# A streaming gradient kernel: one store of each three issued from a second queue, beside a load

## The chip, the cores and the metric

The kernel runs on one core of one Trainium2 chip. The metric is the device time of one execution in microseconds (us), given as the median of several executions. Ratios are the mean time of one kernel's fast runs over the mean time of the other's fast runs of the same rounds, so they are not quite the ratio of the medians quoted beside them. A 95% interval stands behind them where it matters. All profiles below are of executions in the fast state, at a granted clock of 1.00.

## The reference

```python
def setup_inputs():
    return {"x": np.random.randn(8192, 8192).astype(np.float32)}

def reference(x):
    return np.gradient(x, axis=1)
```

Inside a row each output is half the difference of the two neighbours. At the two ends of a row it is the plain difference of the last two elements. The input is 268.44 MB and the output is 268.44 MB; there is little arithmetic beside this traffic.

## The kernel before

The 8192 rows are cut into 32 tiles. A tile has 128 partitions with two whole rows each, which is 64 KB per partition and 8.4 MB in all. Three slots of on-chip memory (SBUF) hold tiles; tile i lives in slot i % 3, and the result is written over the input in the same slot. GpSimd (POOL) computes the row ends, VectorE (DVE) the inside, and either of them places the ends. All loads and all stores are issued by SyncE (SP) on one queue, in the order load, load, load, store, store, store.

```python
x_sets = x.rearrange("(s p t) m -> s p (t m)", p=P, t=R)      # P = 128, R = 2
slots = [pool.tile([P, SH + W], f32, ...) for k in range(NB)]  # NB = 3, W = 2 * 8192

def load(i):
    b = slots[i % NB]
    ins = nc.sync.dma_start(out=b[:, SH : SH + W], in_=x_sets[i])
    loads.append(chain(i, ins, *([stores[i - NB]] if i >= NB else [])))  # waits for the slot's store

for i in range(NB):
    load(i)
for i in range(nsets):                       # nsets = 32
    # ... POOL: ends; DVE: the inside, in place; POOL or DVE: place the ends ...
    ins = nc.sync.dma_start(out=out_sets[i, ...], in_=b[...])
    stores[i] = chain(i, ins, placed)
    if i % NB == NB - 1:                     # after the third store of a group
        for k in range(i + 1, min(i + 1 + NB, nsets)):
            load(k)
```

I call tiles 3g, 3g+1 and 3g+2 a group, with a first, second and third load and store. Each transfer is spread over 16 DMA engines; in the packet records of the trace each engine moves 8 of its 128 partitions, one 64 KB packet per partition. I call these packets rows 0 to 7 of the engine.

## Time and profile before

| | before |
|---|---|
| time, median of 3 runs | 1247.18 us |
| span of the profiled execution | 1245.0 us |
| VectorE busy | 554.8 us, 45% |
| DMA engines busy, mean | 99.8% |
| one group (three loads, three stores), nine groups | 115.96 to 116.68 us, mean 116.3 |

The timeline of one group of the kernel before (start in us, duration or span of the line in us, engine, what; in brackets the idle time of the engine before it and what ended it):

```profile
273.61 39.05 SPq L94 DMA_DIRECT2D out_dram<-slot  x3
275.23 0.20 POOL L70 TENSOR_TENSOR ends<-slot 128x4 f32<-128x4 f32 x1 [1.65 <-DMA slot<-in_x_dram]
...
294.59 0.20 POOL L70 TENSOR_TENSOR ends<-slot 128x4 f32<-128x4 f32 x1 [19.16 <-DMA slot<-in_x_dram]
...
312.11 0.19 POOL L92 COPY slot<-ends 128x4 f32<-128x4 f32 x1 [17.32 <-DVE slot L81]
...
313.93 0.34 SPq L60 DMA_DIRECT2D slot<-in_x_dram  x1
```

The second and third tile of the group become ready for POOL at 275.23 and 294.59, one transfer of 19.3 us apart. The issues of the three stores span 39.05 us from 273.61 on, and the last of them ends at 312.66. When the third is issued, the first two stores still have work for the engines: the loads were done at about 294.2, and two stores are 38.6 us. So the third store arrives a whole transfer before it can start. That reserve is why the engines have no gaps.

The waits of the SP queue itself say the same from another side (what SP waited for: total us, times, longest us):

```profile
SPq L94 <- DVE slot L92: 525.7, 21, 55.9
SPq L60 <- DMA out_dram<-slot: 373.2, 29, 19.2
SPq L94 <- POOL slot L92: 298.8, 12, 36.7
```

SP waits nearly all the time, and none of it costs anything as long as issued work is waiting at the engines.

### The profile page before, as it was taken

What the parts mean: (1) busy time and instruction counts of PE and PEld (TensorE: products, weight loads), DVE (VectorE), ACT (ScalarE), POOL (GpSimd) and SP (SyncE); (2) the same over time, 40 slices, a digit from 0 to 9 for tenths busy, and PEclk for the clock granted to TensorE, in tenths of its full rate; (3) what the DMA queues carried; (4) which work ended last, traced back from release to release, by engine and by line L of the source; (5) the groups of instructions that cost most, each with busy time, mean ns of one, the idle gap of its engine ahead of it and who ended that gap; (6) DMA issues with size and microseconds to landing.
All of it is one profiled execution on the core that took longest, in us unless ns stands there. A gap on an engine that the chain in (4) does not pass through costs nothing.

```text
span 1245.0 us, 241 instructions
## 1 busy us (share of the span) xinstructions
DVE 554.8 (45%) x54; POOL 8.8 (1%) x48
## 2 busy tenths in 40 slices
DVE  2850483079009603850582079009603840591083
POOL 0000000000000000000000000000000000000000
DMA  9999999999999999999999999999999999999999
GB/s 404 438 436 419 425 438 438 438 438 438 434 427 421 436 438 438 436 438 432 432 419 438 436 438 432 436 434 432 423 436 436 436 438 436 430 427 430 436 411 404
DMA packets 9361, 536.88 MB, mean 431 GB/s; under 512 B 1040, under 2 KB 1040, under 8 KB 1040
## 3 DMA queue, kind: packets, MB, share of 16 engines
q1 hardware_dynamic: 9360, 536.88, 99.8%
q14 instruction: 1, 0.01, 0.0%
HBM read 268.44 MB, written 268.44 MB: 431 GB/s over the span
## 4 chain that ended last, share of the span: by engine, by line
another core or an unknown queue 74%; DVE 18%; DMA 3%; issue 2%; POOL 1%; SPq 0%; POOLq 0%
DVE slot L81 18%; DMA slot<-in_x_dram 3%; POOL ends L70 0%; POOL slot L92 0%; SPq L60 0%; DVE slot L92 0%; POOLq L127 0%
## 5 line engine op out<-in xcount | busy, mean ns | idle before, releaser
L81 DVE CUSTOM_DVE_ANT_0 slot<-slot 128x16382 f32<-128x16382 f32 (+1 forms) x33 | 551.3, 16706 | 667.9 <-POOL ends L70 667.9
L70 POOL TENSOR_TENSOR ends<-slot 128x4 f32<-128x4 f32 x32 | 6.3, 198 | 988.8 <-DMA slot<-in_x_dram 988.8
L92 DVE COPY slot<-ends 128x4 f32<-128x4 f32 (+1 forms) x21 | 3.6, 172 | 0.7
L92 POOL COPY slot<-ends 128x4 f32<-128x4 f32 x12 | 2.3, 190 | 207.9 <-DVE slot L81 207.9
L116 POOL MEMSET const-bfloat16-1.0<- 128x1 bf16 x1 | 0.1, 102 | 0.0
L116 POOL MEMSET const-uint8-127<- 128x1 uint8 x1 | 0.1, 102 | 0.0
L116 POOL MEMSET const-float32-0.0<- 128x1 f32 x1 | 0.1, 99 | 0.2 <-issue 0.2
L116 POOL MEMSET const-float32-1.0<- 128x1 f32 x1 | 0.1, 99 | 0.0
## 6 DMA issues: line engine op xcount, KB each, us to landing
out_dram<-slot SPq DMA_DIRECT2D x2, 4096.0 KB, 20.2
slot<-in_x_dram SPq DMA_DIRECT2D x32, 58.0
out_dram<-slot SPq DMA_DIRECT2D x31, 40.3
```

The costliest lines, as they stand in the source:

```text
L70: ins = nc.gpsimd.tensor_sub(out=ends[:, i, :, :], in0=xin[:, :, 1 : m : m - 2], in1=xin[:, :, 0 : m - 1 : m - 2],)
L81: ins = nc.vector._custom_dve(dve_ops.TENSOR_TENSOR_REDUCE_SUB_MAX, out=b[:, c0:c1], in0=b[:, SH + c0 + 1 : SH + c1 + 1], in1=b[:, SH + c0 ...
L92: ins = placer.tensor_copy(out=res[:, :, 0 : m : m - 1], in_=ends[:, i, r : r + nr, :])
L116: nc = _bacc.Bacc("TRN2", target_bir_lowering=False, num_devices=1)
```

## The change

The intent is to let a store run beside the last load of its group, and so to have reads and writes in flight together. The first store of each group goes on the ScalarE (ACT) queue, where it does not have to stand behind the third load. At the end, the last two loads are moved ahead of store 29, which is ready by then, and store 29 runs on the ACT queue beside load 31.

```diff
+    n3 = (nsets - 2) // NB * NB                       # 30
+    next_loads = {i: range(i + 1, i + 1 + NB) for i in range(NB - 1, n3 - NB, NB)}
+    next_loads[n3 - 2] = range(n3, nsets)             # loads 30, 31 right after store 28
...
-                ins = nc.sync.dma_start(
+                queue = nc.scalar if i < n3 and (i % NB == 0 or i == n3 - 1) else nc.sync
+                ins = queue.dma_start(
                     out=out_sets[i, :, r * m : (r + nr) * m], in_=b[:, r * m : (r + nr) * m]
                 )
                 stores[i] = chain(i, ins, placed)
+                if i == n3 - 1:
+                    ... # store 29 waits until load 30 has landed
-            if i % NB == NB - 1:
-                for k in range(i + 1, min(i + 1 + NB, nsets)):
+            if i in next_loads:
+                for k in next_loads[i]:
                     load(k)
```

More of the change, by code (lines that the diff above doesn't have):

```diff
@@ L4 @@
 import concourse.tile as tile
-from concourse import bass_utils, dve_ops
+from concourse import bass_utils, dve_ops, mybir
 from concourse._compat import with_exitstack
@@ L61, in load @@
         loads.append(chain(i, ins, *([stores[i - NB]] if i >= NB else [])))
+    n3 = (nsets - 2) // NB * NB
+    assert nsets - 2 == n3
+    next_loads = {i: range(i + 1, i + 1 + NB) for i in range(NB - 1, n3 - NB, NB)}
+    next_loads[n3 - 2] = range(n3, nsets)
     with tc.manual_schedule():
@@ L97 @@
                 stores[i] = chain(i, ins, placed)
+                if i == n3 - 1:
+                    landed = mybir.DependencyInfo(mybir.DependencyClass.Sync, mybir.DependencyReason.DATA)
+                    tc.add_manual_dep(ins.ins, loads[n3].ins.name, landed, reason="beside the last load")
                 at = [halved]
-            if i % NB == NB - 1:
-                for k in range(i + 1, min(i + 1 + NB, nsets)):
+            if i in next_loads:
+                for k in next_loads[i]:
                     load(k)
```

## The prediction

> **What bounds the kernel now.** I began with the page's busy shares, its queue table and its chain.
>
> ```profile
> DVE 554.8 (45%) x54; POOL 8.8 (1%) x48
> ...
> DMA packets 9361, 536.88 MB, mean 431 GB/s; under 512 B 1040, under 2 KB 1040, under 8 KB 1040
> ...
> q1 hardware_dynamic: 9360, 536.88, 99.8%
> ```
>
> VectorE works 45% of the span; the one DMA queue keeps its 16 engines busy 99.8% of it. So this is a copy kernel: 268.44 MB in, 268.44 MB out, with the arithmetic beside it. The chain is of little use here: 74% of it is put down to an unknown queue, because the semaphores of the slots are reused.
>
> Next I asked for exact cycles of six transfers (three loads, three stores), cut from one tile's first POOL operation to that of the third tile after it.
>
> ```profile
> core 0: us, DVE busy (x) POOL busy (x), PEclk, DMA share, GB/s
> 139.84:255.87 116.03, 52.01 (x5) 0.78 (x4) 1.00 1.00 434
> 255.87:371.99 116.12, 51.84 (x4) 0.97 (x5) 1.00 1.00 433
> 953.95:1070.23 116.28, 52.02 (x5) 0.79 (x5) 1.00 1.00 433
> ```
>
> The DMA share (fifth number after the window) is 1.00 and the rate 433 to 434 GB/s. The packet records say why nothing is left: nearly every packet is a whole 64 KB row, takes 2.418 us (the least and the median; the mean is 2.425), and the next starts 3 ns before it ends, so the pitch is 2.415 us. Each engine has 8 rows of a transfer, so a transfer is 8 x 2.415 = 19.32 us and a cycle 6 x 19.32 = 115.9 us against the 116.03 measured. Loads and stores have the same pitch.
>
> Floor of the whole: 64 tile transfers x 8 rows x 2.415 = 1236.5 us per engine. Add 1.75 us before the first packet, 1.3 us from the last packet to the span's end, and the 2.1 us by which the run (1247.06) exceeds the span (1245.0): 1241.6 us. The kernel stands 5.5 us, 0.4%, above it. Any ordering that moves the same bytes by the same packets lives above 1241.6.
>
> Where the 5.5 us lie, from packets longer than 2.418: an average of 3.65 us per engine, of which 0.6 in the first packets, 1.1 near 41 to 62 us, and the rest in short stretches of up to 0.4 us, mostly in the last packet of a group's third load, just before the first store. The slowest engine lost more than the average, 5.6 us. The other visible hole is at the end:
>
> ```profile
> 1186.42 17.23 DVE L81 CUSTOM_DVE_ANT_0 slot<-slot 128x16382 f32<-128x16382 f32 x1 [59.81 <-POOL ends L70]
> 1203.68 0.17 DVE L92 COPY slot<-ends 128x4 f32<-128x4 f32 x1
> 1203.88 19.93 SPq L94 DMA_DIRECT2D out_dram<-slot  x3
> 1205.53 0.20 POOL L70 TENSOR_TENSOR ends<-slot 128x4 f32<-128x4 f32 x1 [19.14 <-DMA slot<-in_x_dram]
> ...
> GB/s 874 2185 874 437 874 437 0 0 0 0 0 0 0 437 437 437 0 437 0 0 0 0 0 0 0 0 0 0 0 0 0 4806 1748 437 0 0 0 0 0 0
> ```
>
> Store 30 is issued at 1203.88 and its packets start at 1204.72. The last line is the window 1200 to 1206 us in 40 slices by packet starts: almost none between 1202.0 and 1204.6. Twelve engines idle 1.4 to 2.4 us there by the packet records. But the last load's slowest engine ends at 1205.05, after store 30 is there: that engine never waits. All engines finish within 0.2 us of each other at 1243.7.
>
> **What the Trainium skill says.** "DMA: Bandwidth & Descriptors", section "Issuing engines are not separate DMA queues": transfers issued from several engines run on the same 16 DMA engines and interleave, and only issue time is saved. So the ACT queue brings no bandwidth. The trace before has one queue, so it cannot confirm; issue time is 0.34 us a transfer and hidden. Section "Queues, rings and completion order": each engine takes turns between the queues it has work for, packet by packet. I use this for the order of the shared stretch; no run shows it yet. Section "Where 436 GB/s comes from": a ceiling of 435.2 GB/s for the 16 ports. The trace agrees: 16 x 65,536 B / 2.415 us = 434 GB/s. Section "Latency and other measured facts": HBM-to-HBM copies reach a full 214 GB/s each way, so 428 in sum. That speaks against a load and a store overlapping to double the rate, and the trace here has no mixed stretch to test it.
>
> **The change, part by part.** Nothing is removed or added in work: VectorE and POOL have the same 54 and 48 instructions in the same order, and bytes and packet sizes stay. Eleven of 33 store issues move to ACT: ten first stores and store 29.
>
> Part 1, the first store beside the third load. Before, store 3 (issued at 157.57) queued behind load 5. Now it shares the engines with load 5 from about 158.4. The two need 2 x 19.32 = 38.64 us in either order, so store 3 still lands near 197.8, but load 5 lands there too instead of at 178.5. Sum for the engines: 0. The cost is in slack: tile 5 is now ready 19.3 us later, while only store 4 is queued to cover it, and SP issues load 6 only after store 5. Working of that wait, from the slowest engine's last packet of the load to the first packet of store 5: packet end to landing 0.41 (1205.05 to 1205.46), to POOL 0.07, POOL start to store issue 157.57 - 139.84 = 17.73, issue to first packet 0.84 (1203.88 to 1204.72). Sum 19.05 us. Store 4 covers 19.32. Margin 0.27 us, where the kernel before has a whole transfer (some 19 us). So the slowest engine should just not idle, but engines that are ahead by more than 0.27 us will wait, in each of ten groups. Before, a delay on one engine and a delay on another never added up; now each group starts its last store together. Summing the longest excess packet per group (1.0 + 0.3 + 1.1 + 0.1 + 0.3 + 0.2 + 0.4 + 0.8 + 0.8 + 0.8 + 0.7) gives 6.5 us against 5.6 on the slowest engine: about +1 us.
>
> Part 2, taking turns. Each shared stretch goes from a load packet to a store packet 8 times, where before it was once a group. If the excess before a first store (0.17 us per group averaged over engines, first group left out) is the price of that switch, it would be 7 more switches x 0.17 x 10 = 12 us. The next transition, store to load, has no excess packets at all, and some groups show none at load to store either, so I give this a weight of one in six: +2 us.
>
> Part 3, the end. Loads 30 and 31 come straight after store 28, and store 29, ready by then, shares the engines with load 31. Store 30 is computed during that stretch. The hole of about 2 us on most engines closes, but the slowest engine had none; its lead over the others was lost by only 0.3 us (1205.05 against 1204.72). Worth -0.3 us, up to -1.5 if the load is spread evenly.
>
> Sum: +1 + 2 - 0.3, and for the uncertain excesses of the first group (1.1 us in the stretch where store 0 now overlaps load 2) about -1.2: +1.5 us, so 1248.5 us.
>
> **Rivals.** (a) The tight wait becomes the bound. If first packets come later with two queues active, say 1.6 us instead of 0.84 (the very first load took 1.0 to 1.6), each group idles 0.5 us: +5 us in ten groups. For it: 0.27 us is no margin. Against: if on an engine the load's packet goes first, its load ends one packet (2.4 us) earlier. (b) Mixing slows the engines: 428 against 434 GB/s over a third of the time is +6 us; the switch price of part 2 is +12 us; both about +18 us, 1265. (c) Reads and writes overlap in opposite directions: the shared stretches shrink by up to 19 us each and the time falls by over 10%. Against: loads and stores have the same 2.415 us, which looks like the engine's own pace, and the skill's copy figure. (d) Transfers were hidden anyway and only the tail is gained: 1245 to 1247.
>
> **Range and chances.** (d) gives the lower end, and the floor of 1241.6 stands below it; I put it at 1243. Upwards (a) and half of (b) give 1258. Faster by 2% means below 1222, under the floor, so only (c): 0.01. Slower by 2% means over 1272, 25 us, or 2.5 us a group, more than (a) and (b) together: 0.03. Within 2%: 0.96.
>
> **What would show each step.** The packet pitch in shared stretches stays 2.42 us (part 2; near 2.5 would be the switch price, 1.2 would be (c)). Two queues in the queue table, ACT's with 11 of 64 tiles (17% of the bytes), and a total of 99.8% or a little less. Third loads land 38 to 39 us after the second ones. POOL's first operation of a third tile to the next group's: 116.0 to 117 us a cycle; more is rival (a), and then a hole of packet starts just before each third store. The end has no hole before store 30. I am wrong in kind if a cycle is under 115.5 us or over 118 us, and the step that fails is then part 2 or the 19.05 us of part 1.

## More of the kernel before

The prediction shows the busy shares, the queue table, three groups and the end. What matters besides is how far each store is ahead of the time at which an engine could use it.

## The result

| | before | after |
|---|---|---|
| median, 6 runs each | 1247.59 us | 1308.54 us |
| lowest to highest | 1247.16 to 1248.12 | 1287.73 to 1310.3 |
| span of the profiled execution | 1245.0 us | 1304.8 us |

The ratio of fast runs is 1.0398 (95% interval 1.031 to 1.0486): slower. One run took only 1287.73 us. Because of it, four of the other five are over 1.5% above the fastest and so are labelled slow, although the granted clock was 1.00 in all of them; the fast runs are that one and the profiled one of 1306.73. Every single run is at least 39 us slower than the kernel before.

The page of the changed kernel:

```profile
DVE 554.8 (43%) x54; POOL 8.8 (1%) x48
...
DMA packets 9361, 536.88 MB, mean 411 GB/s; under 512 B 1040, under 2 KB 1040, under 8 KB 1040
...
q1 hardware_dynamic: 7776, 444.60, 80.1%
q10 hardware_dynamic: 1584, 92.28, 16.9%
```

The work of VectorE and POOL, the packets and the bytes are unchanged. The two queues together now keep the engines busy 97.0% of a longer span, where it was 99.8%. The rate sinks from 431 to 411 GB/s. The third figure of a queue is the time of its packets. 97.0% of 1304.8 is 1265.7 us per engine, where it was 99.8% of 1245.0, or 1242.5: the packets themselves took 23 us longer. The idle time of an engine rose from 2.5 to 39 us. So there are two halves to explain: **longer packets** and **empty engines**.

Where in time? The windows of the changed kernel, again from POOL's first operation of a group to that of the next (the first is one of 10 us, taken inside a group):

```profile
core 0: us, DVE busy (x) POOL busy (x), PEclk, DMA share, GB/s
213.00:223.00 10.00, 9.10 (x2) 0.00 (x0) 1.00 0.32 138
...
263.27:385.96 122.69, 51.84 (x4) 0.98 (x5) 1.00 0.97 410
385.96:508.44 122.48, 52.01 (x5) 0.79 (x4) 1.00 0.97 411
...
999.15:1122.26 123.11, 52.01 (x5) 0.78 (x4) 1.00 0.97 409
```

Each group takes 122.4 to 123.3 us. In the prediction's three windows it was 116.03 to 116.28, and 115.96 to 116.68 in all nine groups after the first. The loss is the same in every group but the first. The window from 140.00 to 1122.26 holds eight groups and 982.26 us; the eight groups of before, 139.84 to 1070.23, took 930.39. That is 51.9 us. From there to the end it is 182.5 us against 174.8, or 7.7 more. With the 0.2 us before the first window this makes 59.8 us, which is the difference of the spans.

The first of these windows shows what the empty part looks like: for 10 us in the middle of a group, the DMA share is 0.32 and the rate 138 GB/s, while VectorE works 9.10 of the 10 us. It is computing the third tile, and most engines have nothing to do until it is done.

One group of the changed kernel as a timeline:

```profile
403.73 0.34 ACTq L105 DMA_DIRECT2D out_dram<-slot  x1
405.37 0.20 POOL L80 TENSOR_TENSOR ends<-slot 128x4 f32<-128x4 f32 x1 [19.14 <-DMA slot<-in_x_dram]
...
423.06 44.58 SPq L105 DMA_DIRECT2D out_dram<-slot  x2
449.56 0.20 POOL L80 TENSOR_TENSOR ends<-slot 128x4 f32<-128x4 f32 x1 [43.99 <-DMA slot<-in_x_dram]
449.79 17.22 DVE L91 CUSTOM_DVE_ANT_0 slot<-slot 128x16382 f32<-128x16382 f32 x1 [26.76 <-POOL ends L80]
467.08 0.19 POOL L102 COPY slot<-ends 128x4 f32<-128x4 f32 x1 [17.32 <-DVE slot L91]
467.68 21.78 SPq L63 DMA_DIRECT2D slot<-in_x_dram  x3
```

The second tile is ready at 405.37, the third at 449.56. These are 44.2 us, where the prediction said 38 to 39. The issues of the second and the last store span 44.58 us, and the last one ends at 467.64.

The packet starts of the changed kernel from 462 to 469 us, in 40 slices of 0.175 us, show who was waiting:

```profile
GB/s 0 0 0 0 0 0 0 0 1123 375 0 0 0 0 0 0 0 0 0 0 0 374 1123 0 0 0 0 0 0 0 0 0 0 0 0 5243 749 0 0 0
```

A packet of 65,536 bytes in a slice of 0.175 us counts as 374 GB/s, so 1123 is three packets and 5243 is fourteen. Four engines start packets at 463.4 and at 465.8. They are still busy with the second store. Twelve start nothing. At 468.1 all sixteen start together: that is the last store, whose issue ended at 467.64. **Four engines never rest, and twelve wait for them.**

The waits of the SP queue in the changed kernel, to be held against those of before:

```profile
SPq L105 <- DVE slot L102: 623.4, 14, 56.1
SPq L105 <- POOL slot L102: 402.0, 8, 57.7
SPq L63 <- DMA out_dram<-slot: 232.9, 20, 26.8
```

SP now waits 1025.4 us for a tile to be computed (824.5 before) and 232.9 for a store to land (373.2 before). It alone does not say what is wrong, but it shows the turn: the queue lacks computed tiles more often than free slots.

### What the packet records show

The packet records of the trace have the start, duration and queue of every packet on every engine. I put them in chains, one per engine. The following is worked out from them and is not a view of the profile. A normal packet takes 2.418 us; what is above that I call excess.

In one group of the changed kernel a slow engine had this sequence from about 280 us on (A a packet of the first store on ACT's queue, L one of the third load; us):

```
A3.32 L3.33 A3.12 L2.42 A3.06 L2.43 A3.34 L2.42 A2.92 L2.63 A2.42 L3.16
```

The turns are packet by packet, as the prediction said. The packets are not at their usual pace: the excess of these twelve is 5.5 us. The sums for the 16 engines in one group each:

| kernel, group from | excess per engine, us | idle per engine, us |
|---|---|---|
| before, 255.87 | 0.0 to 0.3 | 0.0 |
| after, 385.96, 4 engines | 6.3 to 6.8 | 0.0 |
| after, 385.96, 12 engines | 1.4 to 2.3 | 4.3 to 5.0 |

Excess plus idle is some 6.5 us on every engine. That is the whole loss of the group.

What sets the four apart is where the store comes in. When the first store reaches an engine, the third load is at its start there. If the store's first packet goes out after **two** packets of the load, the excess in the whole stretch is 0.93 us on average (120 stretches of the changed kernel). If it goes out after **one**, it is 5.46 us (26 stretches, 3.2 to 6.25). (These are 146 of 160 stretches; the others are not accounted for.) In the first group all engines had two, and there was no loss. In the second a single engine had one. It was done with the second store 4.8 us and more after the other fifteen, and that alone made the group 123.27 us long. In the later groups three or four had one. They are the engines that run last, so that the arriving store catches them one packet earlier. In the group from 385.96 the first twelve engines were done with the second load between 404.38 and 404.74 us, and had two; the last four were done between 404.76 and 404.87, and had one. A lead of 20 ns made the difference.

### The profile page after: what moved, and what is told of

It reads as the page before. It is cut to its first block, busy times and chain, and to the rows that moved or that the text cites. A ratio compares the mean times of both kernels' runs of the same rounds, so it can differ in the third digit from the quotient of the medians.

```text
span 1304.8 us, 241 instructions
## 1 busy us (share of the span) xinstructions
DVE 554.8 (43%) x54; POOL 8.8 (1%) x48
## 3 DMA queue, kind: packets, MB, share of 16 engines
q10 hardware_dynamic: 1584, 92.28, 16.9%
## 4 chain that ended last, share of the span: by engine, by line
DMA 38%; another core or an unknown queue 32%; DVE 24%; issue 3%; POOL 1%; SPq 0%; POOLq 0%
DMA slot<-in_x_dram 34%; DVE slot L91 24%; DMA out_dram<-slot 4%; POOL ends L80 0%; SPq L105 0%; POOL slot L102 0%; DVE slot L102 0%; SPq L63 0%; POOLq L141 0%
```

## The experiments

Eighteen kernels were run. The texts use letters for the theories. In words: one theory (M in its forms) says that mixing loads and stores costs by itself, because engines get out of step; its first rival says that only the tight wait of the third tile costs; a later one (R) says that a load packet and a store packet slow each other when they are of the same row of an engine and go out one after the other. All results are correct unless the text says that they are wrong. Times are medians of four runs; "before" is the kernel before in the same rounds.

### e1: the first stores alone

```diff
-    next_loads[n3 - 2] = range(n3, nsets)
+    next_loads[n3 - 1] = range(n3, nsets)             # the end as it was
-                queue = nc.scalar if i < n3 and (i % NB == 0 or i == n3 - 1) else nc.sync
+                queue = nc.scalar if i < n3 and i % NB == 0 else nc.sync
                 ... # and the wait of store 29 on load 30 is left out
```

> Part 1 alone (first stores on the ACT queue, the end as in the kernel before). Theory M, out-of-phase mixing plus a wait that passes it on: in the changed kernel eight groups take 122.8 us instead of 116.3, each 6.5 us more, and the end 7.7 us more. Here nine groups should lose 6.5 us each: 1247.5 + 59 = 1306 us (range 1290 to 1312). Rival E, the reordered end is what costs: below 1260.

Measured: 1308.30 us (1303.53 to 1311.74), before 1247.97, ratio 1.0482. The first stores carry the whole loss.

### e2: the end alone

The reverse: only the three edits of the end, with `queue = nc.scalar if i == n3 - 1 else nc.sync`.

> Part 3 alone: only store 29 goes on ACT and loads 30 and 31 go in front of it; all other stores as before. Theory M: one mixed stretch only, so between -1.5 us (the hole before store 30 closed) and +7 us (three engines out of phase): 1246 to 1255. Rival E: most of the 59 us, over 1290.

Measured: 1248.34 us (1248.14 to 1249.1), ratio 1.0004. The new end neither gains nor loses.

### e3: the same order on one queue

```diff
-        for i in range(NB):
+        for i in range(NB - 1):
             load(i)
...
+            if i % NB == 0 and i + 2 < nsets:
+                load(i + 2)                           # third load behind the first store
             if i % NB == NB - 1:
-                for k in range(i + 1, min(i + 1 + NB, nsets)):
+                for k in range(i + 1, min(i + NB, nsets)):
```

This takes the second queue away and keeps the tight wait: load, load, store, load, store, store, all from SP.

> The same late third load without mixing: one queue, in the order load, load, first store, third load, second store, third store. The third store again comes 19.05 us after the third load's last packet with 19.32 us of cover, and the first store has the same 0.27 us of margin. Theory M (the wait is harmless unless an engine was slowed in the mixed stretch): up to 1 us a group for engines that are ahead, 1247 to 1257 us. Rival T, the tight wait by itself costs 6.5 us a group: 1295 or more.

Measured: 1298.67 us, ratio 1.0405, which is a miss for my favourite. One group:

```profile
265.58:387.95 122.37, 51.84 (x4) 0.98 (x5) 1.00 0.97 411
```

That is the same 122.4 us with no packet interleaved; its groups take 119.7 to 122.7 us. By the packet records the loss has another make-up here: every engine has 2.3 to 3.4 us of excess (one has 5.5) and idles 1.7 to 3.0 us. So a third store without reserve can cost this much in another way, and the tight wait could not be dismissed. Experiments e5 to e8 answer to this.

### e4: the first store waits for the second load

```diff
                 stores[i] = chain(i, ins, placed)
+                if i < n3 and i % NB == 0:
+                    ... # this store waits until load i + 1 has landed
```

On each engine the store now comes in a little later, so that two or three packets of the third load are ahead of it.

> The changed kernel with one more wait: a first store on ACT also waits until the second load has landed, about 1.4 us later than it is ready, so that on every engine a packet of the third load is under way before the first packet of the store. Theory M (3 or 4 engines that begin with a store packet while the rest begin with a load packet run out of phase and stretch to 3 to 3.5 us a packet): all engines take turns in phase, stretches of 5 us vanish, a group is 116.3 to 118 us, 1245 to 1265 us in all. Rival T or Q (the tight wait or two queues at all): no change, 1300 or more.

Measured: 1250.41 us (1249.94 to 1251.08), ratio 1.0021. Two windows of it, and the timeline of one group:

```profile
255.44:371.66 116.22, 51.84 (x4) 0.98 (x5) 1.00 1.00 433
838.93:955.51 116.58, 51.84 (x4) 0.98 (x5) 1.00 1.00 432
```

```profile
391.08 0.34 ACTq L105 DMA_DIRECT2D out_dram<-slot  x1
...
408.77 37.23 SPq L105 DMA_DIRECT2D out_dram<-slot  x2
427.91 0.20 POOL L80 TENSOR_TENSOR ends<-slot 128x4 f32<-128x4 f32 x1 [36.64 <-DMA slot<-in_x_dram]
```

The same two queues, the same stores and the same bytes, and the group is back at 116.2 to 116.6 us in these two windows, with a DMA share of 1.00 (116.0 to 117.3 in all full groups after the first). The third tile waits 36.64 us and not 43.99. So the second queue and sharing as such are innocent, and what counts is the moment of arrival, to within one packet.

### e5: more reserve for the third store, the race kept

```diff
-            nr = 1 if last else R
+            nr = 1 if last or (i % NB == NB - 1 and i < n3) else R
```

The changed kernel with the third tile computed and stored in two halves, so that its first half should be stored some 8.5 us sooner. By the trace this came about in five of the ten groups only: there the first half is issued 9.15 us after POOL's start on that tile. In one (tile 29) the stores wait for load 30. In the other four (tiles 8, 11, 23 and 26) POOL places the ends of the first half, and its copy lasts 8.71 us where it was 0.19, until VectorE is done with the second half. There both halves are issued from 17.72 us on, no sooner than in the changed kernel. One of these groups (the copy's line holds both copies, the first from 458.79; the three issues end at 468.34):

```profile
422.13 46.21 SPq L106 DMA_DIRECT2D out_dram<-slot  x3
449.81 0.20 POOL L80 TENSOR_TENSOR ends<-slot 128x4 f32<-128x4 f32 x1 [45.16 <-DMA slot<-in_x_dram]
450.04 17.42 DVE L92 CUSTOM_DVE_ANT_0 slot<-slot 128x8190 f32<-128x8190 f32 x2 [27.93 <-POOL ends L80]
458.79 8.91 POOL L103 COPY slot<-ends 128x2 f32<-128x2 f32 x2 [8.79 <-DVE slot L92]
```

> The changed kernel, first stores on ACT as soon as they are ready (the race with the second load's last packet kept), but every third tile is computed and stored in two halves, so its first half is ready 8.6 us sooner and the last store of a group has 8.9 us of margin instead of 0.27. Theory M1 (the 3 or 4 slow engines are the loss by themselves, 5 to 6 us a group, and the wait only shows it to the rest): still 1285 to 1310. Theory M2 (it takes the wait that makes everyone restart together and puts the same race up again): 1247 to 1262.

Measured: 1302.25 us (1298.99 to 1308.85), before 1247.59, ratio 1.0444. Nearly all the loss stays, and not only where the reserve is missing: the four full groups with reserve after the first take 124.81, 125.55, 117.00 and 121.71 us, 122.3 on average. In the first two of them no engine is idle just before the third store. In the group from 385.09, one without reserve, five engines have an excess of 5.9 to 6.9 us, and the others wait for them. The slow engines cost by themselves, though this run shows it less cleanly than it was meant to.

### e6: no reserve, without the race

The kernel of e4 with a dummy VectorE operation (2480 columns into a scratch tile) ahead of each third tile, which makes its store some 2.6 us later (by the trace the dummy takes 2.74 us, and VectorE begins on the tile 2.84 us after POOL's start, where it was 0.24 in e4).

> The mended order of e4 (the first store waits for the second load, so all engines take turns in phase), with 2.6 us of needless VectorE work put before each third tile, which takes the last store's margin from about 2.5 us back to about 0. Theory T (a store that comes on engines already idle costs the idle time and stretched packets after it): about 2 us a group, 1262 to 1275. Theory M alone (only running out of phase costs): 1249 to 1256.

Measured: 1264.11 us (1263.28 to 1265.41), ratio 1.0133. The tight wait alone costs some 14 us over e4.

These make a square with the changed kernel and e4:

| median us | third store with some reserve | without |
|---|---|---|
| arrival after two or three load packets | 1250.41 (e4) | 1264.11 (e6) |
| arrival left to the race | 1302.25 (e5, reserve in five of ten groups) | 1308.54 (changed kernel) |

### e7: e3 with reserve

The kernel of e3 with the first and third tiles in halves.

> The one-queue order of e3 (load, load, first store, third load, second store, third store), with the first and third tile of each group computed and stored in halves, so that both late stores have 8.9 us of margin instead of 0.27. Theory T (e3 lost its 51 us to the two late stores a group): 1247 to 1255. Rival S (the order itself, with twice as many changes of direction a group, costs): 1275 to 1299.

Measured: 1268.76 us (1267.79 to 1269.77), ratio 1.0169. Reserve brings back 30 of the 51 us of e3, and 21 us stay. Neither theory foretold the middle. Part of it is the edit: as in e5, the first half of a tile is issued no sooner where POOL places it, and that holds for 8 of the 20 halved tiles. The four groups in which both tiles had reserve take 116.8 to 118.2 us, the six others 117.5 to 120.5. So about half of the 21 us (an estimate from these groups) goes with the order, which has more changes of direction per group than before, and the rest with the missing reserve.

### e8: the kernel before with an empty pause

```diff
         loads.append(chain(i, ins, *([stores[i - NB]] if i >= NB else [])))
+        if i >= NB and i % NB == 0:
+            ... # the first load of a group waits until the last store has landed
```

> The kernel before, in its own order and on one queue, but the first load of each group also waits until the last store has landed, so all engines run empty once a group and start again together. Idle time alone: landing 0.41, issue to packets 0.9, so 1.4 us a group plus up to 2 us that the faster engines lose: ten groups, 1262 to 1270. If a restart also stretches the last packet before the next change of direction (0.7 to 1.3 us on nearly all engines, as after each restart in the changed kernel and in e3): about 10 us more, 1270 to 1282.

Measured: 1281.12 us, ratio 1.0270. Two groups:

```profile
142.39:262.26 119.87, 52.02 (x5) 0.79 (x4) 1.00 0.98 420
501.30:620.90 119.60, 52.02 (x5) 0.78 (x4) 1.00 0.99 421
```

These groups are 3.3 and 3.6 us longer than the mean of 116.3. By the packet records, more than the pause itself is lost: the first packet of the first load after the pause takes 0.7 us longer, and the last packet before the next change from loads to stores takes 0.9 to 1.3 us longer (medians of nine groups), on nearly all engines. In the kernel before, which does not run empty, that last packet is usually within some 0.4 us of normal. In the changed kernel the like is seen at the last packet of the third store: in the group from 385.96 it takes 0.4 to 1.1 us longer, 0.67 on average. There it is on all 16 engines, also on the four that had not paused. So about 1 us more at the next change of direction goes with a restart of most engines together, and an engine's own pause is not what it takes. The cause stays open.

### e9: the second store on ACT

The kernel before with `queue = nc.scalar if i % NB == 1 and i < nsets - 1 else nc.sync` for stores.

> Two queues that share the engines, but in one direction: in the kernel before, every second store of a group goes on ACT. It is ready about 0.3 us before the third load's last packet ends, so it runs the same race, and then takes turns with the first store on SP: stores with stores. If engines out of phase lose only where loads meet stores: 1247 to 1253. If two queues out of phase lose in any case: about 5 us a group, 1290 to 1305.

Measured: 1248.98 us (1248.59 to 1249.61), before 1247.83, ratio 1.0006. Two queues that take turns in the same direction cost nothing.

### e10: all loads on SP, all stores on ACT

The kernel before with `nc.scalar.dma_start` for every store.

> All loads on SP, all stores on ACT, order otherwise as before: loads and stores take turns nearly all the time, each transfer takes about 38.6 us, and a slot's round (load 38.6, work 19, store 38.6) is 96 of the 116 us that three tiles of traffic take, so there is slack. If taking turns settles in phase and stays there: 1247 to 1260. If out-of-phase engines keep losing 0.6 to 0.9 us a packet: over 1300.

Measured: 1254.11 us (1250.24 to 1269.15, the longest of them labelled slow, at a granted clock of 1.00), ratio 1.0086 (1.0023 to 1.015). Loads and stores mix through the whole run, and it costs less than 1% by the fast runs. Mixing alone does not make the loss.

### e11: the first store 1.5 us earlier

```diff
                 c0, c1 = r * m + 1, (r + nr) * m - 1
+                c1 -= 1400 if i % NB == 0 and i < n3 else 0
```

The first tile leaves out 1400 columns, so its result is wrong. The store arrives 1.5 us sooner, and all 16 engines are in their first packet of the load. If the loss came from engines out of step, it would vanish; if it came from the order of the packets, all engines would be slow.

> WRONG RESULT ON PURPOSE: the changed kernel, but a group's first tile leaves its last 1400 columns uncomputed, so that its store on ACT comes about 1.5 us sooner, while all 16 engines are still in the second load's last packet (2.42 us long). Then every engine begins with the store packet, all in phase, and the last store's margin stays at 0.27 us. Theory M (what costs is that a few engines are out of phase with the rest): like e6, in phase but tight, 1255 to 1275. Rival F (a store packet ahead of the load packet is what is slow): 1300 or more.

Measured: 1356.42 us (1353.32 to 1358.11), ratio 1.0863. One group:

```profile
276.87:404.92 128.05, 50.39 (x4) 0.98 (x5) 1.00 0.97 393
```

The theory of engines out of step fell here. In this group all 16 engines have an excess of 5.2 to 10.0 us, and all but one idle besides, 1.8 to 7.6 us, because each group waits for the most delayed of them. The group is 11.8 us over 116.3.

From here on the packet records gave a sharper question. I took eight traces (after, e1, e2, e4, e5, e6, e10, e11), found every load packet with a store packet just before and one just after it, and noted which rows of the engine the two stores were, counted from the load's own row k:

| store rows around load row k | pairs | excess of the load and a store packet, ns |
|---|---|---|
| k-3, k-2 | 535 | 9 |
| k-2, k-1 | 3574 | 18 |
| **k-1, k** | 1576 | **744** |
| **k, k+1** | 19 | **694** |
| k+1, k+2 | 456 | 6 |
| k+2, k+3 | 1795 | 5 |

Only where the store of the **same row k** stands next to the load of row k is there an excess. The profiled run of e10 has no such pair. A store that comes in after one load packet gives the order L0 S0 L1 S1 and so on: seven loads with neighbours k-1 and k, so about 7 x 0.744 = 5.2 us (an estimate; 5.46 us measured in the changed kernel). A store that comes in after two gives L0 L1 S0 L2 S1: neighbours k-2 and k-1, and no excess. This is theory R. Load and store have the same shape, so I take row k of an engine to be the same SBUF partition in both, in another slot; no view names the partition of a packet. The Trainium skill's page "DMA: Bandwidth & Descriptors", section "The descriptor swizzle", gives each engine a fixed set of 8 partitions of 128 for its write descriptors; the 8 packets per engine and transfer here agree in number.

### e12, e13 and e14: other partitions, or other rows in DRAM

e12 splits the first store of e11 into two transfers of 64 partitions, the upper half first, so that load and store rows are far apart. e13 is its control, with the lower half first. e14 splits load and store in halves that are swapped in DRAM, so that the SBUF rows meet and the DRAM rows do not.

```diff
+                parts = [(64, 64), (0, 64)] if i < n3 and i % NB == 0 else [(0, P)]   # e12; swapped in e13
```

> WRONG RESULT ON PURPOSE (as e11). A group's first store goes as two transfers of 64 partitions, partitions 64 to 127 first, so that a store packet does not follow the load packet of its own row. Theory R (same row next to each other): the stretching of e11 goes, about 1258 to 1285 us. Rival O (a store one packet behind a load is slow whatever its row): 1335 or more.

> WRONG RESULT ON PURPOSE. Control of e12: the same two transfers of 64 partitions, but partitions 0 to 63 first. If 64 partitions are dealt to the engines four by four, about half of the store packets meet the load packet of their own row. Theory R: between e12 and e11, 1290 to 1340. Rival O: as e12 and e11, 1335 or more. If splitting the store is what helps: as e12.

> WRONG RESULT ON PURPOSE. As e13 in SBUF (partitions 0 to 63 first), but the first tile of a group is loaded with its two halves of rows exchanged, so that in DRAM the store goes to rows 64 to 127 first, as in e12. If the two rows collide in DRAM: near e12. If they collide in SBUF: near e13.

Measured: e12 1384.55 us, e13 1391.84, e14 1608.37 (ratios 1.1115, 1.1147 and 1.2909 to a before of 1248.18). They decide nothing, so rival O is not refuted by them. A window of e14 over its first loads, where no store runs at all, and a later one of whole transfers:

```profile
2.50:42.00 39.50, 0.00 (x0) 0.00 (x0) 1.00 0.92 189
43.00:62.00 19.00, 15.94 (x2) 0.20 (x1) 1.00 0.90 390
```

The transfers of 64 partitions move 189 GB/s; by the packet records each of their 64 KB packets takes 5.12 us, where 2.42 is usual. So they are slow alone, and the question was covered by another cost. I had not foreseen it.

### e15 and e16: the store's rows ahead of the load's

The kernel of e11 with 5900 and with 3700 columns left out (wrong again). The store then arrives so early that its rows should be ahead of the load's: by two and more in e15, by just one in e16.

> WRONG RESULT ON PURPOSE. As e11, but 5900 columns of a group's first tile are left out, so its store comes about 6.2 us before it does in the changed kernel and runs a row or two ahead of the load (store rows k+1 and k+2 around load row k). Theory R: pairs cost next to nothing, in phase but tight: 1255 to 1275. Rival A (the earlier the store, the worse; e11 was worse than the changed kernel): over 1356.

> WRONG RESULT ON PURPOSE. As e15 with 3700 columns left out, about 3.9 us sooner than in the changed kernel: the store's row k goes directly before the load's row k (store rows k and k+1 around load row k). Theory R: as slow as e11, 1330 to 1375. If only a store behind its load is slow: 1255 to 1275.

Measured: e15 1269.04 us (1267.47 to 1270.58), before 1247.50, ratio 1.0173. An even earlier store than e11's, with 87 us less time. The pairs are at k+2, k+3 (715 of them, excess 1 ns), as R asks. e16 took 1274.47 us (1268.16 to 1280.99), ratio 1.0217, and R's expectation of a slow run was missed: I had the arrival wrong by one packet. The pairs turned out at k+1, k+2 (888, excess 6 ns), so by R there is no stretch, and there was none. The order k, k+1 on all engines was not reached; it has only the 19 pairs of the table. What e15 and e16 lose against before is not stretch of such pairs; the third store's wait, as in e6, is the likely part. One group of each agrees: the mixed stretch has at most 0.2 us of excess per engine, while in the whole group engines idle up to 0.9 us (e15) and 2.0 us (e16) and have 1.2 to 3.1 us of excess, where in e6 it is up to 1.3 and 1.2 to 2.5.

### e17 and e18: rows far apart in DRAM

```diff
-    x_sets = x.rearrange("(s p t) m -> s p (t m)", p=P, t=R)
+    x_sets = x.rearrange("(g p q t) m -> g q p (t m)", p=P, q=4, t=R)
```

The same for the output. Four tiles are interleaved, so the rows of one tile lie 256 KB apart in DRAM, and a load and a store of neighbouring partitions are no longer in neighbouring DRAM. e17 does this to e11 (wrong for the 1400 columns), e18 to the kernel before (correct).

> WRONG RESULT ON PURPOSE. e11 (every engine has the store's row right after the load's same row) with four tiles interleaved in DRAM, so that the same partition of the two tiles is 128 KB, and a multiple of 32 MB, apart. If the rows collide in DRAM: near e18 plus 10 to 25 us. If they collide in SBUF: the stretch stays, e18 plus about 110 us.

> Control of e17: the kernel before with the same interleaved layout in DRAM. Its packets are still whole 64 KB rows, so 1245 to 1260 if the 256 KB step between partitions costs nothing; if it is much slower, e17 is judged against this.

Measured: e18 1249.09 us, ratio 1.0015; the layout costs nothing of note. e17 1355.53 us (1353.06 to 1356.55), ratio 1.0870, as slow as e11, and its 1062 pairs at k-1, k have 723 ns of excess. So the distance in DRAM, which differs here, is hardly the cause. That leaves the SBUF side, where the two packets touch the same partition; this is inferred, not shown. No run separates the same partition from the same place in the two transfers, or from a store that is one packet behind its load whatever its row (rival O): with whole transfers they go together, and e12 to e14, which were to part them, failed.

## Why the prediction was wrong

The record said 1248.5 us, in a range from 1243 to 1258. It came out at 1308.54 us, 60 us higher.

**What held.** The second queue brought no bandwidth, and the engines take turns between the queues packet by packet. ACT's queue has 16.9% of the engines' time (17% of the bytes expected). VectorE and POOL are unchanged. Part 3, the end, was given -0.3 us; e2 against before (1248.34 and 1247.97) shows no difference clear of noise. Rival (c), overlap of reads and writes, did not happen. The sign to look for was also right: "more is rival (a), and then a hole of packet starts just before each third store", and for a cycle over 118 us "the step that fails is then part 2 or the 19.05 us of part 1". It was part 2; the 19.05 us held.

**Part 2, taking turns, is the step that failed.** It gave +2 us, one sixth of a switch price of 12, because the transitions of before had little excess. The transitions before are between transfers, though, where the last row of one meets the first of the other. They could not show what happens when equal rows meet. In place of the +2 there is 0.74 us for a load and a store packet of the same row next to each other, 5.5 us per group on each engine where the store came in after one load packet (pair table; e11 makes it so on all engines, e15 on none). The rate per packet was taken for a constant of the engine, and it depends on the order.

**Part 1, "So the slowest engine should just not idle, but engines that are ahead by more than 0.27 us will wait", was right in its words and wrong in its size.** It gave about +1 us in all. In place of this: in most groups three or four of 16 engines, in the second group one, are late by the stretch of part 2, the third load is complete only when the last of them has landed, and its store is issued some 17.8 us after that. The sum of 19.05 us held: in the group from 385.96 the last engine is done with the third load at 449.11, and the first packet of the third store starts at 468.14, 19.03 us later. The four late engines do not idle, and the other twelve wait 4.3 to 5.0 us. Then comes about 1 us that goes with the common restart, of which e8 shows the like in the kernel before: the last packet of the third store takes 0.7 us longer, and some 0.3 us are spread. So 5.5 + 0.7 + 0.3 is some 6.5 us a group, and eight groups lost 51.9 us as measured. The end lost 7.7, because the stretch of load 29 beside store 27 leaves three engines behind: the last packets of 13 engines end at about 1296.5 us and those of three at about 1303.4.

**The same margin was overlooked in a second place.** The sum of 19.05 us also runs from the end of the first load to the first packet of its store, and the second load takes 19.32. So the first store, too, arrives some 0.27 us before the last engine is done with the second load, while the engines that lead are already in the third. The prediction used the margin for the wait of the third store alone. Here it decides the order of the packets: leads of some tenths of a us, out of a packet of 2.42, put an engine on one side or the other. It may also explain the one run of 1287.73 us, if the race falls out differently from run to run; only the profiled run has packet records.

**The rivals.** (a) had 5 us for the tight wait; e6 shows some 14. (b) had 18 for the mixing and the switches; the true mixing is nearly free (e10, e4), and one order of rows is dear. Together they could not reach 60.

**What stays open.** Why neighbouring packets of the same row slow each other, and whether it is the SBUF partition that counts or only the store's lag of one packet (rival O); whether k, k+1 on all engines is as slow as k-1, k; why the next change of direction after a common restart takes longer; and why those engines are the last. No version beat the kernel before: e4 takes the harm away and is still 0.2% slower. By the prediction's floor of 1241.6 us there were 0.5% to gain at most.

## What to carry to other kernels

When a streaming kernel already keeps its DMA engines 99.8% busy on one queue, issuing part of the transfers from another queue can only change the order, and the order can cost: look at which row's load and store meet on one engine, and make a store start a safe number of packets away from its row's load, by a wait on a landed transfer as in e4. A transfer is complete only when its slowest engine is done, so a delay on four engines of sixteen, or on one as in the second group, is a delay on all as soon as a computation waits for the whole tile. With a margin that is small against one packet, leads of 20 ns decide, and the profile of the old kernel cannot tell how it falls.

## What the Trainium skill lacked or had wrong

- "DMA: Bandwidth & Descriptors", section "Issuing engines are not separate DMA queues", says that transfers from several engines interleave and only issue time is saved. It lacks that interleaving can cost: the same stores issued from ACT beside a load took 1308.30 us against 1247.97 (e1), while 1248.98 (e9) and 1250.41 (e4) show it free in other orders.
- The same page, "Queues, rings and completion order", gives turns by packet, with a packet of about 9 to 17 descriptors typical. Here the turns went by single 64 KB rows of 2.42 us. It lacks that a queue that arrives on a busy engine gets its first turn after one or two packets, by the engine's lead (20 ns in one group), which decided 5.5 us or 0.9 us of excess per group and engine.
- No page has the cost of a load and a store packet of the same row of an engine next to each other (taken to be the same SBUF partition, which is not shown): 744 ns a pair (1576 pairs), and at most 18 ns at the other distances of the table but k, k+1.
- No page has the cost of starting again after all engines ran empty: beyond the pause, 0.7 us at the first packet and 0.9 to 1.3 us at the last one before the next change of direction, on nearly all engines (e8).
